# Summing the high and low parts of the PEER gates in PSUM: two 128-column products per token, one copy for four tokens

## The chip, the cores and the metric

One core of one Trainium2 chip runs the whole program. The metric is the device time of one execution in microseconds (us), the median of several runs. Engines are named as in the profile: PE is TensorE (its matrix products), PEld are PE's weight loads, DVE is VectorE, ACT is ScalarE, POOL is GpSimd, SP is SyncE, which issues most of the transfers.

## What is computed

The reference is two transformer blocks for 256 tokens of width 2048 in float32. The change touches the last layer, a PEER layer: every token picks 128 experts (8 heads of 16) out of 16384 = 128 x 128 by product keys, each with a gate, and sums their contributions.

```python
expert = jnp.take_along_axis(cand_idx, top_pos, axis=-1)
gate = jax.nn.softmax(top_s, axis=-1)
u = jnp.take(peer_u, expert, axis=0)
act = jax.nn.gelu(jnp.einsum('chkd,cd->chk', u, zc))
v = jnp.take(peer_v, expert, axis=0)
w = (gate * act.astype(jnp.float32)).astype(zc.dtype)
return jnp.einsum('chk,chkd->cd', w, v).astype(zc.dtype)
```

The kernel gathers nothing. It computes the gelu of **all** 16384 experts for all tokens (the stage that streams `peer_u`), builds a dense gate matrix with one 128 x 128 square of gates per token, multiplies the two, and forms the dense sum over all experts (the stage that streams `peer_v`).

## The kernel before

Every large weight matrix streams through the same loop (`Weights.take`, L125): SP loads 1 MB into one of 3 buffers `raw`; for each half of it, a chunk of 1024 columns, ACT writes the rounded high part `hi` (L140, format fp32r) and DVE the rest `lo` (L143), each into one of 4 buffers; then PE multiplies. A float32 product is made of three fp32r products: high by high, high by low, low by high (`unit_a`, L165 to L167). In the `peer_u` stage there are 32 units of 8 chunks. A chunk takes 24 products of 128 x 128 weights with 256 moving columns.

The gates are built beside this, as background work. `bg` is a list of (cost, function); after the split of each chunk, `take` calls `pump(1400)` (L144, L92), which takes entries from the front for as long as its budget is above 0 and subtracts each entry's cost:

```python
    def pump(budget):
        while bg and budget > 0:
            cost, fn = bg.popleft()
            fn()
            budget -= cost
```

So these costs decide how much gate work stands beside one chunk, and the scheduler then sets the order on each engine.

The gate work is done in 32 groups of 8 tokens. For a group, DVE makes four tiles of 1024 elements per partition, listed at a cost of 1250 each: `ha` (L1025, the one-hot rows of the first key), `he` (L1030, one-hot of the second key), and the two halves of `hb` (L1036, `he` times the high part and times the low part of the gates). In these tiles a partition is one of the token's 128 picked experts, so that the product of `ha` and `hb` over the partitions puts each gate at its place in the square. `meet` (L1038) makes that product on PE: one product per token, with `ha` of the token as weights and both parts of `hb` as 256 moving columns; a PSUM tile `gps` (one of 4 with the tag `tr`) takes two tokens. `store` (L1046) adds the two parts: ACT copies the high half to the tile `gst` (L1054) and DVE adds the low half to it (L1055), at a listed cost of 700. `gst` holds 32 tokens, in one of 2 buffers; after four groups a POOL-issued transfer writes it to memory (L1057). The entries are listed one group late: the products of group g stand between the one-hots of group g + 1 (L1059 to L1070). From the costs, a group before takes four calls of `pump`, so four chunks.

At the last unit (L1093) what is left of the list is emptied, and the `peer_v` stage reads the gates back.

Of the kernel before, what the change touches and what calls it, by code (L numbers as in the profile page):

```python
# [10 lines left out]
F32 = mybir.dt.float32  # L11
# [3 lines left out]
AF = mybir.ActivationFunctionType  # L15
ALU = mybir.AluOpType
# [29 lines left out]
def build(tc, t, out, dbg=None, stop=None):  # L46
# [4 lines left out]
    V, A, P, T = nc.vector, nc.scalar, nc.gpsimd, nc.tensor  # L51
# [36 lines left out]
    bg = deque()  # L88
# [199 lines left out]
    ps = tc.tile_pool(name="ps1", bufs=1, space=PSUM)  # L288
    psx = ExitStack()
    ps = psx.enter_context(ps)  # L290
# [51 lines left out]
    for g in range(4):  # L342
        z = xTs[g // 2][:, 4 * (g % 2):4 * (g % 2) + 4, :]
# [479 lines left out]
    for u in range(2):  # L823
# [3 lines left out]
        for g in (2 * u, 2 * u + 1):  # L827
# [7 lines left out]
            for jt in range(2):  # L835
                yp = ps.tile([128, 512], F32, tag="tr", name="yp", bufs=4)
                for i in range(2):
                    T.matmul(yp[:, :256], pw[:, g, i, 128 * jt:128 * jt + 128], dT[:, i, :],  # L838
                             start=(i == 0), stop=(i == 1))
                k = 2 * g + jt  # L840
# [14 lines left out]
    for n in range(4):  # L855
        acc = unit_b(ps, w, yh, yl, 16)
        for c in range(2):
            z = x2[:, c, 512 * n:512 * n + 512]
# [29 lines left out]
    st = [tk.tile([128, 16, 128], F32, name=f"st{c}") for c in range(2)]  # L888
# [113 lines left out]
    G = {}  # L1002
# [10 lines left out]
    NT = 8  # L1013
# [8 lines left out]
    def hot_a(g):  # L1022
        a = G["hot"].tile([128, 1152], F32R, tag="ha", name="ha")[:, 16:1040].rearrange("p (t k) -> p t k", t=NT)
        hot[g] = [a]
        V.tensor_tensor(a, iota8(), over(slotT[:, 0, :], g), op=ALU.is_equal)  # L1025

    def hot_e(g):
        e = G["hot"].tile([128, NT, 128], F32, tag="he", name="he", bufs=1)
        hot[g].append(e)
        V.tensor_tensor(e, iota8(), over(slotT[:, 1, :], g), op=ALU.is_equal)  # L1030

    def hot_b(g, i):
        if i == 0:
            hot[g].append(G["hot"].tile([128, NT, 2, 128], F32R, tag="hb", name="hb"))
        x = gateh.bitcast(F32) if i == 0 else gatel
        V.tensor_tensor(hot[g][2][:, :, i, :], hot[g][1], over(x, g), op=ALU.mult)  # L1036

    def meet(g, p):  # L1038

        a, _, b = hot[g]  # L1040
        o = ps.tile([128, 2, 2, 128], F32, tag="tr", name="gps", bufs=4)
        for j in range(2):
            T.matmul(o[:, j, :, :], a[:, 2 * p + j, :], b[:, 2 * p + j, :, :], start=True, stop=True)  # L1043
        hot[g, p] = o

    def store(g, p):  # L1046
        o = hot.pop((g, p))
        if g % 4 == 0 and p == 0:
            G["st"] = G["stage"].tile([128, NK, 32], F32, tag="gst", name="gst")
        k = NT * (g % 4) + 2 * p  # L1050
        z = G["st"][:, :, k:k + 2]
        h, l = o[:, :, 0, :], o[:, :, 1, :]
        h, l = h.rearrange("p t i -> p i t"), l.rearrange("p t i -> p i t")
        A.activation(z, h, AF.Copy)  # L1054
        V.tensor_tensor(z, l, z, op=ALU.add)  # L1055
        if g % 4 == 3 and p == NT // 2 - 1:
            nc.gpsimd.dma_start(gD[g // 4], G["st"].rearrange("p i t -> p (i t)"))  # L1057

    for g in range(S // NT + 1):  # L1059
        first, last = g == 0, g == S // NT  # L1060
        for i, fn in enumerate((lambda g=g: hot_a(g), lambda g=g: hot_e(g),
                                lambda g=g: hot_b(g, 0), lambda g=g: hot_b(g, 1))):
            if not last:
                bg.append((1250, fn))
            if not first:
                bg.append((0, lambda g=g, i=i: meet(g - 1, i)))
                if i:
                    bg.append((700, lambda g=g, i=i: store(g - 1, i - 1)))
        if not first:
            bg.append((700, lambda g=g: store(g - 1, 3)))  # L1070

    opt["budget"], opt["pool"] = 1400, 0
    wsp = lslot("lhi", "wsp", (4, 4, 256), off=16)
# [203 lines left out]
```

## Time and profile before

| | us |
|---|---|
| median of 3 runs | 2879.12 (2878.49 to 2879.72) |
| the profiled execution | 2881.8 |
| its span in the trace | 2880.0 |
| PE busy in the span | 2840.0 (99%) |
| DVE busy in the span | 1896.9 (66%) |
| ACT busy in the span | 1327.6 (46%) |

The profile shows one execution: each instruction with start, duration and what it waited for. A product's recorded duration covers its way through the array, and the next starts long before it ends; what PE spends on one is the distance between starts, called its step here. PE and PEld overlap in the same way.

### The profile page before, as it was taken

The numbers are of one execution on the slowest core, as the hardware profiler recorded it, in microseconds if no ns is written. First come the engines' busy times: TensorE is split into PE (matmuls) and PEld (weight loads), VectorE is DVE, ScalarE is ACT, GpSimd is POOL, SyncE is SP. The second block draws the span as 40 slices with busy tenths as digits, with TensorE's granted clock in tenths as the row PEclk, the third lists the DMA queues.
The fourth block names the chain that finished last, engine by engine and source line by source line (L and its number), as shares of the span: only waits on it lengthen the run. The fifth ranks groups of instructions, "written<-read, shape, count | busy, mean of one in ns | idle before, by whom it ended". The sixth has DMA issues, their size and how long they took to land.

```text
span 2880.0 us, 45191 instructions
## 1 busy us (share of the span) xinstructions
PE 2840.0 (99%) x18950; PEld 2596.6 (90%) x18950; DVE 1896.9 (66%) x2531; ACT 1327.6 (46%) x1638; POOL 33.0 (1%) x45
## 2 busy tenths in 40 slices
PE   8999999999999999999999999999999999999998
PEld 8887799999998888888999999999998888888886
DVE  7976665555554447856997988995445555555555
ACT  6226554444444445545444555544444444444443
POOL 0000000000000000000000000000000000000000
PEclk9999999999999999999999999999999999999999
DMA  6444555555565556465456667668667677767663
GB/s 239 165 148 145 205 199 197 191 193 195 198 220 190 194 197 219 147 219 212 173 214 221 227 231 263 231 256 300 219 219 277 236 241 244 241 239 247 236 223 141
DMA packets 120253, 615.72 MB, mean 214 GB/s; under 512 B 10320, under 2 KB 43216, under 8 KB 54768
## 3 DMA queue, kind: packets, MB, share of 16 engines
q1 hardware_dynamic: 116656, 574.16, 57.0%
q0 software_dynamic: 3392, 38.67, 3.4%
q8 instruction: 148, 2.42, 0.3%
q14 instruction: 57, 0.47, 0.0%
HBM read 570.85 MB, written 41.94 MB: 213 GB/s over the span
## 4 chain that ended last, share of the span: by engine, by line
PE 71%; issue 25%; DVE 3%; ACT 1%; DMA 0%; POOL 0%; SPq 0%; DVEq 0%; POOLq 0%
PE acc L167 16%; PE acc L166 16%; PE acc L165 16%; PE acc L180 6%; PE acc L179 6%; PE acc L181 6%; PE acc L189 3%; PE gps L1043 1%; DVE lo L143 1%; PE acc L198 0%; PE scp L922 0%; PE yp L838 0%; DMA raw<-w_in 0%; PE sp L515 0%; PE tsp L249 0%
## 5 line engine op out<-in xcount | busy, mean ns | idle before, releaser
L143 DVE TENSOR_TENSOR lo<-raw,hi 128x1024 fp32r<-128x1024 f32 (+1 forms) x968 | 1176.0, 1218 | 845.3 <-ACT hi L140 844.3
L140 ACT ACTIVATE hi<-raw 128x1024 fp32r<-128x1024 f32 (+1 forms) x968 | 1022.7, 1058 | 1345.6 <-PE acc L166 671.1
L167 PE MATMUL acc<-znh,lo 128*128 128x256 f32 x2048 | 564.7, 277 | 2.0 <-DVE lo L143 1.8
L165 PE MATMUL acc<-znh,hi 128*128 128x256 f32 x2048 | 565.5, 277 | 0.0
L166 PE MATMUL acc<-znl,hi 128*128 128x256 f32 x2048 | 565.5, 277 | 0.0
L1122 PE MATMUL o<-hi,wsp 128*128 128x512 f32 x2048 | 547.7, 389 | 0.0
L165 PE MATMUL acc<-lhi,hi 128*128 128x256 f32 x1856 | 514.6, 278 | 9.5 <-ACT hi L140 9.1
L166 PE MATMUL acc<-llo,hi 128*128 128x256 f32 x1856 | 514.6, 278 | 0.9 <-DVE llo L253 0.9
L167 PE MATMUL acc<-lhi,lo 128*128 128x256 f32 x1856 | 512.9, 277 | 1.3 <-DVE lo L143 1.2
L1122 PEld LDWEIGHTS o<-hi,wsp 128*128 128x128 f32 x2048 | 384.3, 188 | 79.8
L167 PEld LDWEIGHTS acc<-znh,lo 128*128 128x128 f32 x2048 | 383.3, 188 | 3.4 <-DVE lo L143 3.4
L165 PEld LDWEIGHTS acc<-znh,hi 128*128 128x128 f32 x2048 | 385.2, 188 | 0.0
L166 PEld LDWEIGHTS acc<-znl,hi 128*128 128x128 f32 x2048 | 384.5, 188 | 0.0
L165 PEld LDWEIGHTS acc<-lhi,hi 128*128 128x128 f32 x1856 | 350.4, 189 | 9.9 <-ACT hi L140 9.1
L166 PEld LDWEIGHTS acc<-llo,hi 128*128 128x128 f32 x1856 | 350.6, 189 | 1.4 <-DVE llo L253 1.4
L167 PEld LDWEIGHTS acc<-lhi,lo 128*128 128x128 f32 x1856 | 349.4, 189 | 2.2 <-DVE lo L143 2.2
L1122 PE MATMUL o<-lo,wsp 128*128 128x512 f32 x1024 | 315.4, 389 | 0.0
L1122 PEld LDWEIGHTS o<-lo,wsp 128*128 128x128 f32 x1024 | 192.2, 188 | 39.9
L180 PE MATMUL acc<-lo,acth 128*128 128x512 f32 x352 | 136.9, 389 | 0.0
L179 PE MATMUL acc<-hi,acth 128*128 128x512 f32 x352 | 136.9, 389 | 0.0
L181 PE MATMUL acc<-hi,actl 128*128 128x512 f32 x352 | 136.9, 389 | 0.0
L180 PE MATMUL acc<-lo,lhi 128*128 128x512 f32 (+1 forms) x352 | 136.7, 389 | 0.0
(338 smaller groups left out, 2728.0 us busy)
## 6 DMA issues: line engine op xcount, KB each, us to landing
raw<-peer_u SPq DMA_DIRECT2D x128, 1024.0 KB, 4.9
raw<-peer_v SPq DMA_DIRECT2D x128, 1024.0 KB, 5.9
raw<-w_gu SPq DMA_DIRECT2D x88, 1024.0 KB, 4.9
raw<-w_in SPq DMA_DIRECT2D x47, 1024.0 KB, 4.9
raw<-w_down SPq DMA_DIRECT2D x44, 1024.0 KB, 4.9
raw<-w_out SPq DMA_DIRECT2D x32, 1024.0 KB, 4.9
raw<-peer_wq SPq DMA_DIRECT2D x16, 1024.0 KB, 4.8
hD<-hg SPq DMA_DIRECT2D x32, 512.0 KB, 3.1
```

The lines of the kernel that those rows point to most:

```text
L140: A.activation(hi[:, :m], raw[:, o:o + m], AF.Copy)
L143: e.tensor_tensor(lo[:, :m], raw[:, o:o + m], hi[:, :m].bitcast(F32), op=ALU.subtract)
L165: T.matmul(o, hi[:, c], xh[:, kt, :], start=(kt == 0 and m % 2 == 0), stop=False)
L166: T.matmul(o, hi[:, c], xl[:, kt, :], start=False, stop=False)
L167: T.matmul(o, lo[:, c], xh[:, kt, :], start=False, stop=(kt == nkt - 1 and m % 2 == 1))
L179: T.matmul(o, xh[:, k, s], hi, start=(kt == 0), stop=False)
L180: T.matmul(o, xh[:, k, s], lo, start=False, stop=False)
L181: T.matmul(o, xl[:, k, s], hi, start=False, stop=(kt == nkt - 1))
L189: T.matmul(acc[m // 2][:, m % 2, :], v[:, m * 128:m * 128 + 128], x(kt), start=(kt == 0 and m % 2 == 0), stop=(kt == nkt - 1 and m % 2 == 1))
L1043: T.matmul(o[:, j, :, :], a[:, 2 * p + j, :], b[:, 2 * p + j, :, :], start=True, stop=True)
L1122: T.matmul(acc[c][o // 512 + q], x[:, s], v[:, 512 * q:512 * q + 512], start=st, stop=sp)
```

## The change

`meet` is called twice for a group instead of four times. It makes, for each of four tokens, two products of 128 moving columns, first with the high part and then with the low part of `hb`, which add up at the same place of a PSUM tile; the tile now holds four tokens. The weights of the two products are the same. `store` is one ACT copy of 512 elements per partition; DVE's addition is gone. The listed cost of `store` is 0 instead of 700.

```diff
@@ -1038,22 +1038,20 @@
     def meet(g, p):
 
         a, _, b = hot[g]
-        o = ps.tile([128, 2, 2, 128], F32, tag="tr", name="gps", bufs=4)
-        for j in range(2):
-            T.matmul(o[:, j, :, :], a[:, 2 * p + j, :], b[:, 2 * p + j, :, :], start=True, stop=True)
+        o = ps.tile([128, 4, 128], F32, tag="tr", name="gps", bufs=4)
+        for j in range(4):
+            for i in range(2):
+                T.matmul(o[:, j, :], a[:, 4 * p + j, :], b[:, 4 * p + j, i, :],
+                         start=(j == 0 and i == 0), stop=(j == 3 and i == 1))
         hot[g, p] = o
 
     def store(g, p):
         o = hot.pop((g, p))
         if g % 4 == 0 and p == 0:
             G["st"] = G["stage"].tile([128, NK, 32], F32, tag="gst", name="gst")
-        k = NT * (g % 4) + 2 * p
-        z = G["st"][:, :, k:k + 2]
-        h, l = o[:, :, 0, :], o[:, :, 1, :]
-        h, l = h.rearrange("p t i -> p i t"), l.rearrange("p t i -> p i t")
-        A.activation(z, h, AF.Copy)
-        V.tensor_tensor(z, l, z, op=ALU.add)
-        if g % 4 == 3 and p == NT // 2 - 1:
+        k = NT * (g % 4) + 4 * p
+        A.activation(G["st"][:, :, k:k + 4], o.rearrange("p t i -> p i t"), AF.Copy)
+        if g % 4 == 3 and p == 1:
             nc.gpsimd.dma_start(gD[g // 4], G["st"].rearrange("p i t -> p (i t)"))
 
     for g in range(S // NT + 1):
@@ -1062,12 +1060,12 @@
                                 lambda g=g: hot_b(g, 0), lambda g=g: hot_b(g, 1))):
             if not last:
                 bg.append((1250, fn))
-            if not first:
-                bg.append((0, lambda g=g, i=i: meet(g - 1, i)))
+            if not first and i % 2 == 0:
+                bg.append((0, lambda g=g, i=i: meet(g - 1, i // 2)))
                 if i:
-                    bg.append((700, lambda g=g, i=i: store(g - 1, i - 1)))
+                    bg.append((0, lambda g=g: store(g - 1, 0)))
         if not first:
-            bg.append((700, lambda g=g: store(g - 1, 3)))
+            bg.append((0, lambda g=g: store(g - 1, 1)))
 
     opt["budget"], opt["pool"] = 1400, 0
     wsp = lslot("lhi", "wsp", (4, 4, 256), off=16)
```

The scheduler places the rows of each engine. On DVE, in the middle of the gate stage, before; from one `he` (L1030) to the next is one group, with `lo` (L143) of the chunks of the weight stream between:

```order
L1030 TENSOR_TENSOR he<-cst,slotT 128x1024
L143 TENSOR_TENSOR lo<-raw,hi 128x1024 x2
L1055 TENSOR_TENSOR gst<-gps,gst 128x128x2 x2
L143 TENSOR_TENSOR lo<-raw,hi 128x1024
L1055 TENSOR_TENSOR gst<-gps,gst 128x128x2
L1025 TENSOR_TENSOR ha<-cst,slotT 128x1024
L1036 TENSOR_TENSOR hb<-he,gateh 128x8x128
L1036 TENSOR_TENSOR hb<-he,gatel 128x8x128
L143 TENSOR_TENSOR lo<-raw,hi 128x1024
L1055 TENSOR_TENSOR gst<-gps,gst 128x128x2
```

and now:

```order
L1025 TENSOR_TENSOR ha<-cst,slotT 128x1024
L143 TENSOR_TENSOR lo<-raw,hi 128x1024
L1030 TENSOR_TENSOR he<-cst,slotT 128x1024
L143 TENSOR_TENSOR lo<-raw,hi 128x1024
L1036 TENSOR_TENSOR hb<-he,gateh 128x8x128
L1036 TENSOR_TENSOR hb<-he,gatel 128x8x128
```

A group stood among four chunks of the stream and now stands among two; the four additions (L1055) are gone.

On PE, the products of the gates between two chunks, with buffer numbers, before (L1043):

```order
L167 MATMUL acc_15585<-znh_12208,lo_15623 128x256
L1043 MATMUL gps_15660<-hb_15549,ha_15479 128x256 x2
L1043 MATMUL gps_15665<-hb_15549,ha_15479 128x256 x2
L165 MATMUL acc_15584<-znh_12208,hi_15656 128x256
L166 MATMUL acc_15584<-znl_12209,hi_15656 128x256
```

and now (the same line is L1044 of the changed file):

```order
L165 MATMUL acc_15303<-znh_12208,hi_15476 128x256
L166 MATMUL acc_15303<-znl_12209,hi_15476 128x256
L167 MATMUL acc_15303<-znh_12208,lo_15477 128x256
L1044 MATMUL gps_15521<-hb_15406,ha_15363 128x128 x8
L165 MATMUL acc_15302<-znh_12208,hi_15517 128x256
```

The eight products of a group, of 256 columns, are now sixteen of 128 columns, in the same stream of products of 256 columns.

## Rows read from the trace of the kernel before

**Rows 1.** The page, parts 1 and 4: busy us of each engine, the chain's shares.
```profile
PE 2840.0 (99%) x18950; PEld 2596.6 (90%) x18950; DVE 1896.9 (66%) x2531; ACT 1327.6 (46%) x1638; POOL 33.0 (1%) x45
...
PE 71%; issue 25%; DVE 3%; ACT 1%; DMA 0%; POOL 0%; SPq 0%; DVEq 0%; POOLq 0%
```

**Rows 2.** Timeline of PE at the gate products: start us, us, and xcount merged.
```profile
1596.14 0.84 PE L1043 MATMUL gps<-hb,ha 128*128 128x256 f32 x6
1596.82 0.28 PE L167 MATMUL acc<-znh,lo 128*128 128x256 f32 x1
```

**Rows 3.** Stretches inside the peer_u stage: us, each engine's busy us (instructions), clock, DMA.
```profile
1700.00:1800.00 100.00, 100.00 (x885) 100.00 (x884) 89.34 (x103) 50.35 (x78) 1.06 (x2) 1.00 0.70 252
...
1965.00:2060.00 95.00, 95.00 (x840) 95.00 (x840) 49.23 (x41) 42.79 (x46) 0.00 (x0) 1.00 0.80 280
```

**Rows 4.** Timeline of POOL: two of the eight stores of gates.
```profile
1687.17 0.54 POOL L1057 DMA_DIRECT2D gD<-gst  x1 [46.36 <-DVE gst L1055]
1734.32 0.53 POOL L1057 DMA_DIRECT2D gD<-gst  x1 [46.60 <-DVE gst L1055]
```

**Rows 5.** Groups by line and shape, 1590 to 1965: busy us, mean ns, idle before.
```profile
L143 DVE TENSOR_TENSOR lo<-raw,hi 128x1024 fp32r<-128x1024 f32 x128 | 153.9, 1218 | 21.6 <-ACT hi L140 21.6
...
L1055 DVE TENSOR_TENSOR gst<-gps,gst 128x256 f32<-128x256 f32 x128 | 50.8, 420 | 0.0
L1054 ACT ACTIVATE gst<-gps 128x256 f32<-128x256 f32 x128 | 47.1, 400 | 0.0
...
L1036 DVE TENSOR_TENSOR hb<-he,gatel 128x1024 fp32r<-128x1024 f32 x32 | 39.0, 1218 | 0.0
L1036 DVE TENSOR_TENSOR hb<-he,gateh 128x1024 fp32r<-128x1024 f32 x32 | 39.0, 1217 | 0.0
L1030 DVE TENSOR_TENSOR he<-cst,slotT 128x1024 f32<-128x1024 f32 x31 | 37.6, 1214 | 0.0
L1025 DVE TENSOR_TENSOR ha<-cst,slotT 128x1024 fp32r<-128x1024 f32 x30 | 36.7, 1224 | 16.9 <-PE gps L1043 16.9
```

**Rows 6.** Waits, 1590 to 1965: us in total, times, longest us.
```profile
ACT hi L140 <- PE acc L166: 168.4, 111, 1.7
DVE lo L143 <- ACT hi L140: 21.6, 33, 1.4
```

**Rows 7.** Groups by line: ScalarE's copy of 512 elements out of PSUM, at the key scores.
```profile
L923 ACT ACTIVATE st<-scp 128x512 f32<-128x512 f32 x8 | 4.6, 598 | 4.7 <-PE scp L922 4.5
```

**Rows 8.** Timeline of PE in the last stage, 512 columns.
```profile
2300.07 1.07 PE L1122 MATMUL o<-hi,wsp 128*128 128x512 f32 x4
```

**Rows 9.** The page, part 5: the 512-column products and their weight loads.
```profile
L1122 PE MATMUL o<-hi,wsp 128*128 128x512 f32 x2048 | 547.7, 389 | 0.0
...
L1122 PEld LDWEIGHTS o<-hi,wsp 128*128 128x128 f32 x2048 | 384.3, 188 | 79.8
```

**Rows 10.** Timeline of PE at the key scores, plain f32 of 128 columns.
```profile
1370.51 1.95 PE L922 MATMUL scp<-kk,qTu 128*128 128x128 f32 x16
```

**Rows 11.** Timeline of PE around four one-column records of plain f32.
```profile
36.85 0.39 PE L167 MATMUL acc<-lhi,lo 128*128 128x256 f32 x2
37.08 0.50 PE L336 MATMUL rtk<-ones,xsq 128*128 128x1 f32 x4
37.44 0.36 PE L165 MATMUL acc<-lhi,hi 128*128 128x256 f32 x1
37.65 0.28 PE L166 MATMUL acc<-llo,hi 128*128 128x256 f32 x1
```

**Rows 12.** Timeline of PE's weight loads in the same stretch.
```profile
36.97 0.53 PEld L336 LDWEIGHTS rtk<-ones,xsq 128*128 128x128 f32 x4
```

**Rows 13.** DMA issues of the whole run: xcount, KB each, median us to landing.
```profile
raw<-peer_u SPq DMA_DIRECT2D x128, 1024.0 KB, 4.9
...
gD<-gst POOLq DMA_DIRECT2D x8, 2048.0 KB, 12.3
```

## The prediction

> **What bounds the kernel now.** I read the page first, then stretches of the stage in which the change lies, then the groups, waits and timelines of that stage. PE is busy for 99% of the span and the chain of waits runs through PE, with DVE at 3% and ACT at 1% of it [rows 1]. Busy time of PE alone proves little, since its records overlap, so the step matters, the distance between two starts. In the gate stage six gate products start between 1596.14 and 1596.82 [rows 2]: 0.68 / 6 = 0.1133 us for a product of 256 columns. After the stage 840 products lie in 95 us [rows 3], 0.1131 us each. So with the gate work beside it PE ran as densely as without it; no stall of PE is left there for the change to win back.
>
> A group of gates before takes four chunks: 4 x 24 x 0.1133 + 8 x 0.1133 = 10.88 + 0.91 = 11.79 us of PE. Two stores of gates, four groups apart, are 1734.32 - 1687.17 = 47.15 us apart [rows 4], which is 4 x 11.79: PE sets the pace exactly. DVE is close behind it. Per group it has four `lo` (1.218 us), one each of `ha`, `he` and the two `hb` (1.224 + 1.214 + 1.217 + 1.218 = 4.87 us) and four additions of 0.420 us [rows 5]: 4.87 + 4.87 + 1.68 = 11.43 us, and 89.34 of 100 us busy in mid-stage [rows 3]. What DVE idles there, it waits for others: 16.9 us before `ha` for PE [rows 5], 21.6 us before `lo` for ACT, which waits for PE to free `hi` [rows 6]. It is slack, though little.
>
> **What goes: DVE and ACT work.** 128 additions of 0.420 us leave DVE, 53.8 us. 128 copies of 0.400 us leave ACT [rows 5] and 64 of 512 elements come; the nearest row, a copy of the same size out of PSUM, took 0.598 us [rows 7]: 51.2 us becomes 38.3 us. Neither was on the path, so I price both gains at nothing. ACT is half idle in the stage [rows 3]; per group it will have two `hi` and two copies, about 3.3 us of 7.3 us.
>
> **What comes: the products on PE.** 256 products of 256 columns become 512 of 128. The old ones took 256 x 0.1133 = 29.0 us. The trace has no fp32r product under 256 columns, so the step has to be bounded.
> - From below: half of 0.1133 us, if columns alone counted. Then 512 x 0.0567 = 29.0 us, a difference of 0. Columns do set the step of long products: four of 512 columns take 1.07 us [rows 8] with a record of 0.389 us [rows 9], so (1.07 - 0.389) / 3 = 0.227 us, twice that of 256.
> - From above: a plain f32 product of 128 columns, which leaves two records. Sixteen records take 1.95 us [rows 10]; less a last record of some 0.28 us, 1.67 / 15 = 0.111 us each, 0.223 us a product. Then 114.2 us, a difference of +85.
> - Between them: every product loads its own weights. The page counts 2048 loads for 2048 products, though in that line two neighbours share their weights [rows 9]; so the second product of a token will load again. How fast loads follow one another is seen where columns cost nothing: two products of a single column, four records, stand among the stream. From 36.85 to 37.65 there are two stream records, the four, and one more [rows 11]: 0.80 / 7 = 0.114 us each, no faster than 256 columns. The four loads take 0.53 us [rows 12], with 0.188 us for one [rows 9]: (0.53 - 0.188) / 3 = 0.114 us apart. I take 0.112 us, between this and the 0.111 us of the 128-column records: the weight load sets the floor, and halving the columns buys nothing.
>
> So PE gets 512 x 0.112 = 57.3 us for 29.0 us: **+28.3 us**, on the bounding engine, with nothing to hide it.
>
> The Trainium skill (TensorE: Matmul & The Clock Gate, section Back-to-back issue gap) gives about 81 ns per product at 128 columns and about 131 ns at 512 for a sustained stream of load and product pairs. As an estimate by its 81 ns, PE's term would be 512 x 0.081 - 29.0 = +12.5 us, and the time 2892 us if PE alone set it. The trace differs from that section where both can be compared: 512 columns take 227 ns here [rows 8], so the row decides.
>
> **What moves: the pace of the gate work.** With `store` listed at 0, a group takes two calls of the pump instead of four, and the order on DVE shows it: two `lo` beside the four gate tiles. DVE then needs 2 x 1.218 + 4.87 = 7.31 us per group, and PE 2 x 24 x 0.1133 + 16 x 0.112 = 5.44 + 1.79 = 7.23 us. DVE, ahead before, becomes the slower by a hair. Paced by DVE the 32 groups take 233.9 us. The same 64 chunks with the old products were 64 x 2.72 + 29.0 = 203.1 us of PE. That is **+30.8 us**: PE's +28.3 us and 2.5 us of waiting for `lo` or `hb`. It also means that a quicker product helps little: anything under 0.117 us (7.31 - 5.44 = 1.87 us over 16) is paced by DVE. The other 64 chunks of the old stage run afterwards at PE's bare 2.72 us, so nothing is lost or won there.
>
> On the queues the work comes closer together. The store of gates on POOL lands in 12.3 us [rows 13] and comes every 4 x 7.31 = 29.2 us, with two `gst` buffers. SP's 1 MB loads land in 4.9 us [rows 13] and are wanted once per 7.31 us. The copies queue in front of `hi` on ACT and wait for the products, but four `hi` buffers lie between. I price these at nothing; without that cover, they would add to rival one.
>
> The sum against the profiled execution: 2881.8 + 30.8 = 2912.6 us. It stands 2.7 us above the median of the runs, so 2879.1 + 30.8, about **2910 us**, 1.1% slower. A measurement of this kernel can tell about 0.2% (5.8 us) from no change. The forecast's own range is 2905 (PE alone, a step of 0.109 us) to 2916 (0.114 us, and a few us of waits).
>
> **Rivals.**
> 1. DVE's waits stay. It waited 16.9 us in total for PE before `ha` [rows 5]; before, that was slack. If it waits as long with DVE setting the pace, the group takes 7.31 + 0.53 = 7.84 us, and 32 x 7.84 - 203.1 = +47.8 us: 2927. For it: the two engines are nearly level, and each waits for the other in turn. Against: there are two `ha` buffers, so a `ha` needs only the products of the group before last to be done. Chance 0.10.
> 2. fp32r under 256 columns runs as plain f32, in two passes: 0.223 us [rows 10], +85 us, 2964. Against: the fp32r rows cost what their columns cost, and nothing in the trace shows a second kind. Chance 0.06.
> 3. The products go at the columns' rate, 0.0567 us, and DVE's lead covers part of its pace. The lead is at most four `lo` tiles, 4 x 2.72 = 10.9 us, of 30.8 us: at least +20 us, 2899. The weight loads [rows 11, 12] speak against it. Chance 0.04.
> 4. Not slower. The same quick products, and DVE no longer binding: PE needs 5.44 + 0.91 = 6.35 us per group, so this decides from 6.35 / 6 = 1.06 us per DVE operation downwards, now that the additions have gone. Time 2879. DVE's tiles of this size took 1.214 to 1.224 us, all of them [rows 5]. Chance 0.02.
>
> **How the numbers follow.** Forecast 0.78, rivals 0.10, 0.06, 0.04 and 0.02. The range, 2902 to 2928, holds the forecast with its bounds and reaches up to rival 1; it leaves out rivals 2 to 4, 0.12, and some tail. All cases but rival 4 are slower by more than 0.2%: slower 0.98, same 0.01, faster 0.01.
>
> **What would show it.** Gate products of 128 columns with steps near 0.112 us, PEld as dense as PE, and 512 of each. Stores of gates some 29 us apart: 29.0 means PE's pace (7.23 x 4 = 28.9), 29.2 DVE's, 31.4 rival 1, 36 rival 2 (4 x 9.0), 25.4 rival 4. DVE near 100% busy for some 234 us from 1596, and the stage then running bare to its end. The prediction is wrong if the step lies far from 0.112 us while the time is as forecast (then DVE was the bound), or if the stage shows PE waiting much longer than 5 us in all.

## The result and the profile after

The changed kernel took 2909.26 us (2908.40 to 2909.83, 4 runs) against 2879.42 us of the kernel before (4 runs beside it): a ratio of 1.0103, 95% interval 1.0091 to 1.0115. That is 29.8 us more, in the range of the prediction and 0.7 us under its figure. The profiled executions differ less, 2908.4 against 2881.8 us, because that of before lies 2.7 us above its median and that of after 0.9 us under its own. Most of that lies ahead of the first gate product (see the last section).

The page of the changed kernel, parts 1 and 4:

```profile
PE 2866.7 (99%) x19206; PEld 2623.8 (90%) x19206; DVE 1860.3 (64%) x2403; ACT 1322.7 (46%) x1574; POOL 33.0 (1%) x45
...
PE 71%; issue 24%; DVE 2%; ACT 1%; DMA 1%; POOL 0%; SPq 0%; DVEq 0%; POOLq 0%
```

Against [rows 1], PE has 19206 - 18950 = 256 more products and as many more weight loads, and 26.7 us more busy time; DVE has 36.6 us less, ACT 4.9 us less. The chain still runs through PE at 71%, and DVE's share of it went from 3% to 2%: what DVE and ACT were relieved of shows in their busy time and hardly on the path.

The timeline of PE at the gate products (start us, us, records merged):

```profile
1649.44 0.90 PE L1044 MATMUL gps<-hb,ha 128*128 128x128 f32 x7
1650.18 0.33 PE L167 MATMUL acc<-znh,lo 128*128 128x256 f32 x1
1650.35 0.28 PE L165 MATMUL acc<-znh,hi 128*128 128x256 f32 x1
```

This answers to [rows 2]. Seven products of 128 columns start at 1649.44; the next product of the stream starts at 1650.18 and the one after it at 1650.35. Those eight, seven short ones and one of 256 columns, take 0.91 us, 0.114 us each. In [rows 2] the same engine spent 0.1133 us on twice the columns.

Stretches of the stage (us, then busy us of PE, PEld, DVE, ACT and POOL with instructions, clock, DMA):

```profile
1620.00:1800.00 180.00, 180.00 (x1588) 180.00 (x1587) 173.28 (x150) 84.22 (x112) 3.20 (x6) 1.00 0.65 240
1840.00:1960.00 120.00, 120.00 (x1061) 120.00 (x1061) 57.51 (x48) 52.96 (x57) 0.00 (x0) 1.00 0.69 243
```

PE is full in the gate stage and behind it, as in [rows 3], at 180 / 1588 = 0.1134 and 120 / 1061 = 0.1131 us per product. But of every 64 products 16 now belong to the gates, where it was 8 of 104.

The stores of gates on POOL:

```profile
1646.70 0.54 POOL L1055 DMA_DIRECT2D gD<-gst  x1 [28.66 <-ACT gst L1053]
...
1762.88 0.53 POOL L1055 DMA_DIRECT2D gD<-gst  x1 [28.48 <-ACT gst L1053]
```

Four stores, sixteen groups, lie in 1762.88 - 1646.70 = 116.18 us: 29.05 us per store and 7.26 us per group, where [rows 4] gave 47.15 us and 11.79 us. Two chunks of the stream are 5.44 us of it, so 16 products took 1.82 us, **0.114 us each**.

Groups of the gate stage by line and shape, 1590 to 1820 (xcount, busy us, mean ns of one, idle before):

```profile
L143 DVE TENSOR_TENSOR lo<-raw,hi 128x1024 fp32r<-128x1024 f32 x64 | 78.3, 1223 | 11.4 <-ACT hi L140 11.2
...
L1044 PE MATMUL gps<-hb,ha 128*128 128x128 f32 x512 | 65.8, 267 | 0.0
L1044 PEld LDWEIGHTS gps<-hb,ha 128*128 128x128 f32 x512 | 63.3, 191 | 0.0
L1036 DVE TENSOR_TENSOR hb<-he,gatel 128x1024 fp32r<-128x1024 f32 x32 | 39.0, 1220 | 0.0
L1053 ACT ACTIVATE gst<-gps 128x512 f32<-128x512 f32 x64 | 37.9, 593 | 14.1 <-PE gps L1044 14.1
...
L1025 DVE TENSOR_TENSOR ha<-cst,slotT 128x1024 fp32r<-128x1024 f32 x30 | 36.8, 1226 | 0.3
```

Against [rows 5], the additions are gone and the copies of 512 elements took 593 ns, as [rows 7] had it. DVE's 16.9 us of waiting for PE before `ha` has become 0.3 us. Its wait for `hi` before `lo`, 21.6 us for 128 `lo` in [rows 6], is 11.2 us for 64: DVE still idles. The timeline of DVE shows how long one of its tiles holds it:

```profile
1645.81 1.22 DVE L1025 TENSOR_TENSOR ha<-cst,slotT 128x1024 fp32r<-128x1024 f32 x1
1646.95 1.22 DVE L143 TENSOR_TENSOR lo<-raw,hi 128x1024 fp32r<-128x1024 f32 x1
1648.09 1.22 DVE L1030 TENSOR_TENSOR he<-cst,slotT 128x1024 f32<-128x1024 f32 x1
1649.57 1.23 DVE L143 TENSOR_TENSOR lo<-raw,hi 128x1024 fp32r<-128x1024 f32 x1 [0.27 <-ACT hi L140]
1650.71 1.22 DVE L1036 TENSOR_TENSOR hb<-he,gateh 128x1024 fp32r<-128x1024 f32 x1
1651.85 1.22 DVE L1036 TENSOR_TENSOR hb<-he,gatel 128x1024 fp32r<-128x1024 f32 x1
```

The records last 1.22 us, but two that follow without a wait start 1.14 us apart (1646.95 to 1648.09, 1650.71 to 1651.85). So DVE's records overlap, as those of PE do, and the step of such a tile is 1.14 us.

### The profile page after: what moved, and what is told of

The parts are those of the page before. It is cut to its first block, busy times and chain, and to the rows that moved or that the text cites. A ratio compares the mean times of both kernels' runs of the same rounds, so it can differ in the third digit from the quotient of the medians.

```text
span 2906.6 us, 45562 instructions
## 1 busy us (share of the span) xinstructions
PE 2866.7 (99%) x19206; PEld 2623.8 (90%) x19206; DVE 1860.3 (64%) x2403; ACT 1322.7 (46%) x1574; POOL 33.0 (1%) x45
## 4 chain that ended last, share of the span: by engine, by line
PE 71%; issue 24%; DVE 2%; ACT 1%; DMA 1%; POOL 0%; SPq 0%; DVEq 0%; POOLq 0%
PE acc L165 16%; PE acc L167 16%; PE acc L166 16%; PE acc L181 6%; PE acc L180 6%; PE acc L179 6%; PE acc L189 2%; PE gps L1044 2%; DVE lo L143 1%; DMA raw<-w_out 0%; ACT hi L140 0%; PE scp L922 0%; PE yp L838 0%; PE acc L198 0%; DMA raw<-w_in 0%
## 5 line engine op out<-in xcount | busy, mean ns | idle before, releaser
L143 DVE TENSOR_TENSOR lo<-raw,hi 128x1024 fp32r<-128x1024 f32 (+1 forms) x968 | 1180.0, 1220 | 937.0 <-ACT hi L140 935.5
```

The costliest lines, as they stand in the source:

```text
L143: e.tensor_tensor(lo[:, :m], raw[:, o:o + m], hi[:, :m].bitcast(F32), op=ALU.subtract)
```

## The experiments

Three readings were set against each other. **W**: a product's step at 128 columns is set by the load of its weights, so the added products cost all of the loss. **D**: the gate work was squeezed between two chunks and DVE sets the pace there. **C**: columns alone count, and the loss has another cause. The diff of the first run is against the kernel before, those of the others against the changed kernel.

### The split alone

```diff
         for j in range(2):
-            T.matmul(o[:, j, :, :], a[:, 2 * p + j, :], b[:, 2 * p + j, :, :], start=True, stop=True)
+            for i in range(2):
+                T.matmul(o[:, j, i, :], a[:, 2 * p + j, :], b[:, 2 * p + j, i, :],
+                         start=(j == 0 and i == 0), stop=(j == 1 and i == 1))
```

> The kernel before, with only the products split: each product of 256 columns is two of 128 columns with the same weights, into the two halves of the same tile; copy, addition, listed costs and the pace of four chunks per group stay. Theory W (the weight load sets a product's step, about 0.112 us at 128 columns): 512 x 0.112 - 29.0 = +28 us, ratio 1.010, about 2908 us; stores of gates 4 x (10.88 + 1.79) = 50.7 us apart. Theory D (the change is slower because the gate work was squeezed among two chunks and DVE sets the pace there): nothing is squeezed here, ratio 1.000 to 1.002. Theory C (columns alone count, step 0.057 us): ratio 1.000.

Measured: ratio 1.0104 (1.0087 to 1.0121), 2910.56 us, the whole of the loss with nothing of the rest of the change. Its stores of gates:

```profile
1693.52 0.54 POOL L1059 DMA_DIRECT2D gD<-gst  x1 [50.04 <-DVE gst L1057]
1744.34 0.53 POOL L1059 DMA_DIRECT2D gD<-gst  x1 [50.28 <-DVE gst L1057]
```

50.82 us apart, against 47.15 us in [rows 4]: 3.67 us for 32 products more, 0.115 us for each added one. C falls on this run, and so does D as the cause of the loss, since nothing was squeezed here. Whether DVE costs the changed kernel 2 or 3 us on top is left to the runs below.

### The pace alone

```diff
-        o = ps.tile([128, 4, 128], F32, tag="tr", name="gps", bufs=4)
-        for j in range(4):
-            for i in range(2):
-                T.matmul(o[:, j, :], a[:, 4 * p + j, :], b[:, 4 * p + j, i, :],
-                         start=(j == 0 and i == 0), stop=(j == 3 and i == 1))
-        hot[g, p] = o
+        hot[g, p] = []
+        for q in range(2):
+            o = ps.tile([128, 2, 2, 128], F32, tag="tr", name="gps", bufs=4)
+            for j in range(2):
+                n = 4 * p + 2 * q + j
+                T.matmul(o[:, j, :, :], a[:, n, :], b[:, n, :, :], start=True, stop=True)
+            hot[g, p].append(o)
...
-        A.activation(G["st"][:, :, k:k + 4], o.rearrange("p t i -> p i t"), AF.Copy)
+        for q in range(2):
+            A.activation(G["st"][:, :, k + 2 * q:k + 2 * q + 2],
+                         o[q][:, :, 0, :].rearrange("p t i -> p i t"), AF.Copy)
```

> The changed kernel's listing with the old products: 256 columns per token, two tokens per tile, two copies per store and no addition; the low part is left out of the sum (it is computed on PE, not copied). The order on DVE gives 2.5 chunks per group on average. Theory W: PE does what it did before, 2.5 x 2.72 + 0.91 = 7.71 us per group, and nothing else counts: ratio 1.000, 2879 to 2881 us. Theory D: DVE at 1.22 us for each of 6.5 tiles needs 7.93 us per group, so 32 x 0.22 = +7 us, ratio 1.0025 or more. Theory C says as W.

Measured: 0.9996 (0.9987 to 1.0006), 2880.19 us. Taking the additions away and drawing the gate work together, here among 2.5 chunks a group and not 2, neither gains nor costs anything that the interval shows, and D's 1.0025 lies outside it.

### Twice as many products again

```diff
             for i in range(2):
-                T.matmul(o[:, j, :], a[:, 4 * p + j, :], b[:, 4 * p + j, i, :],
-                         start=(j == 0 and i == 0), stop=(j == 3 and i == 1))
+                for s in (slice(0, 64), slice(64, 128)):
+                    T.matmul(o[:, j, s], a[:, 4 * p + j, :], b[:, 4 * p + j, i, s],
+                             start=(j == 0 and i == 0 and s.start == 0),
+                             stop=(j == 3 and i == 1 and s.start == 64))
```

> The changed kernel with each product of 128 columns made as two of 64 columns, 1024 in all, same weights. Theory W: 1024 x 0.112 - 29.0 = +86 us over before, ratio 1.030, about 2965 us. If a product costs columns plus a fixed part (0.112 = 0.053 + 0.059), 64 columns cost 0.086 us: 88 - 29 = +59 us, ratio 1.020. Theory C: as the changed kernel, 1.010. Theory D: the pace of DVE hides it only up to 0.117 us per two products, so it says nothing of its own here.

Measured: 1.0314 (1.0297 to 1.0332), 2972.23 us, so +90.4 us. A fixed part plus columns (1.020) is excluded; the 1024 products cost as much each as the 512. The 4 to 5 us over W's 86 us can be found in the trace:

```profile
1600.00:1604.00 4.00, 4.00 (x23) 4.00 (x23) 3.44 (x4) 0.94 (x2) 0.00 (x0) 0.57 0.46 195
1604.00:1608.00 4.00, 4.00 (x38) 4.00 (x37) 2.60 (x3) 2.39 (x4) 0.00 (x0) 1.00 0.36 128
1872.00:1876.00 4.00, 4.00 (x38) 4.00 (x37) 1.23 (x1) 2.02 (x3) 0.00 (x0) 1.00 0.48 199
1876.00:1880.00 4.00, 4.00 (x24) 4.00 (x24) 0.00 (x0) 0.60 (x1) 0.53 (x1) 0.59 0.15 66
```

In the profiled execution the granted clock fell twice to its lower level (1.2 GHz) for some 3 us, with 0.57 and 0.59 on average in these stretches and 1.00 beside them. Each time PE had just made a long row of gate products of 64 columns, 28 and 48 of them one behind the other, where a row has 16 in most groups. That cost 15 and 14 products of the stream, 3.3 us. The rest is the step, which is 0.1133 us and not W's 0.112: 1024 x 0.1133 - 29.0 = +87.0 us, with 3.3 us +90.3 us.

### One DVE tile more per group

```diff
-        V.tensor_tensor(e, iota8(), over(slotT[:, 1, :], g), op=ALU.is_equal)
+        for _ in range(2):
+            V.tensor_tensor(e, iota8(), over(slotT[:, 1, :], g), op=ALU.is_equal)
```

> The changed kernel with one more DVE tile per group (the one-hot of the second key is made twice). The order on DVE gives 8/3 chunks per group. PE needs 2.67 x 2.72 + 16 x 0.1133 = 9.07 us per group. Theory W (PE alone; DVE's step from start to start is 1.135 us in the trace, so 7.67 x 1.135 = 8.70 us): as the changed kernel, ratio 1.010, within 2 us of it. Theory D (1.22 us a tile, 7.67 x 1.22 = 9.35 us, 0.28 us per group over PE): +9 us on the changed kernel, ratio 1.0135.

Measured: 1.0107 (1.0090 to 1.0124), 2911.83 us, as the changed kernel. The stores tell more sharply than the time:

```profile
1666.47 0.54 POOL L1056 DMA_DIRECT2D gD<-gst  x1 [35.90 <-ACT gst L1054]
...
1775.57 0.53 POOL L1056 DMA_DIRECT2D gD<-gst  x1 [36.14 <-ACT gst L1054]
```

Three intervals between stores, twelve groups, take 109.10 us, 9.09 us per group: PE's 9.07 us, not D's 9.35 us. With 32 more DVE tiles the stage still ran at PE's pace.

### A slower pace for the same work

```diff
-                    bg.append((0, lambda g=g: store(g - 1, 0)))
+                    bg.append((1400, lambda g=g: store(g - 1, 0)))
...
-            bg.append((0, lambda g=g: store(g - 1, 1)))
+            bg.append((1400, lambda g=g: store(g - 1, 1)))
```

> The changed kernel with the listed cost of a store at 1400 instead of 0, so that a group stands among three chunks instead of two; the work is the same. Theory W (PE alone, 0.113 us for each of 512 loads): as the changed kernel, ratio 1.010. Theory D (DVE set the changed kernel's pace): with 7 tiles per group for three chunks DVE has slack even at 1.22 us (8.54 against 9.97 us of PE), so 2 to 3 us less than the changed kernel, ratio 1.0095 or less.

Measured: 1.0101 (1.0086 to 1.0117), 2910.10 us. It agrees with W; the interval is too wide to exclude D's 1.0095 by itself.

### Half the columns, the same number of products

```diff
-            for i in range(2):
-                T.matmul(o[:, j, :], a[:, 4 * p + j, :], b[:, 4 * p + j, i, :],
-                         start=(j == 0 and i == 0), stop=(j == 3 and i == 1))
+            T.matmul(o[:, j, :], a[:, 4 * p + j, :], b[:, 4 * p + j, 0, :], start=(j == 0), stop=(j == 3))
```

> The changed kernel with the product of the high part alone: 256 products of 128 columns, half the columns of the kernel before; the low part of the gates is left out of the sum. Theory W: 256 loads as before, 256 x 0.112 = 28.7 us for 29.0 us, ratio 1.000, 2879 to 2882 us. Theory C (columns count): 256 x 0.057 = 14.5 us, ratio 0.995, about 2866 us. 2.5 chunks per group keep DVE out of it: 6.5 x 1.135 = 7.38 us against 7.7 us of PE under theory W.

Measured: 1.0002 (0.9993 to 1.0011), 2882.21 us. Half of the gate columns of the kernel before are gone and nothing is gained; C's 0.995 lies far outside. In fp32r the number of products, each with its load, sets the time, here 256 as before.

Loads and products are equal in number in all these runs, so the counts alone can't tell the load from another fixed cost of an fp32r product. The timeline of the changed kernel speaks for the load. Here one gate product stands alone in the stream (PE first, then the loads):

```profile
1648.39 0.22 PE L1044 MATMUL gps<-hb,ha 128*128 128x128 f32 x1
1648.45 0.33 PE L165 MATMUL acc<-znh,hi 128*128 128x256 f32 x1
1648.62 0.28 PE L166 MATMUL acc<-znl,hi 128*128 128x256 f32 x1
```

```profile
1648.28 0.19 PEld L1044 LDWEIGHTS gps<-hb,ha 128*128 128x128 f32 x1
1648.39 0.19 PEld L165 LDWEIGHTS acc<-znh,hi 128*128 128x128 f32 x1
1648.50 0.19 PEld L166 LDWEIGHTS acc<-znl,hi 128*128 128x128 f32 x1
1648.62 0.19 PEld L167 LDWEIGHTS acc<-znh,lo 128*128 128x128 f32 x1
```

The product behind it starts after 0.06 us, about what 128 columns cost at the rate of the 512-column products (0.227 / 4 = 0.057 us). But its record is 0.05 us longer than its neighbours', and the one behind it starts only after 0.17 us, while the loads keep steps of 0.11 to 0.12 us. So the short product gave PE free early, and what it saved was lost again to the pace of the loads. The ends of PE's records are modelled, and no run made several products from one load: this is an argument, not a proof.

### The same products in bf16

```diff
-        a = G["hot"].tile([128, 1152], F32R, tag="ha", name="ha")[:, 16:1040].rearrange("p (t k) -> p t k", t=NT)
+        a = G["hot"].tile([128, 1152], BF16, tag="ha", name="ha")[:, 16:1040].rearrange("p (t k) -> p t k", t=NT)
...
-            hot[g].append(G["hot"].tile([128, NT, 2, 128], F32R, tag="hb", name="hb"))
-        x = gateh.bitcast(F32) if i == 0 else gatel
+            hot[g].append(G["hot"].tile([128, NT, 2, 128], BF16, tag="hb", name="hb"))
+        x = gateh if i == 0 else gatel
```

The high part `gateh` is in bf16 as well (one ScalarE copy writes it), and `gatel` is the rest.

> The changed kernel with the operands of the gate products in bf16 instead of fp32r: the one-hots exactly, the gates as a bf16 high part and the rest rounded to bf16. Same 512 products of 128 columns. If the load's time hangs on the operand's width (theory W with a load of about half, step 0.057 to 0.060 us): 512 x 0.058 = 29.7 us, ratio 1.000, about 2881 us; DVE at 1.135 us stays under PE on average (6.4 x 1.135 = 7.26 us against 7.45 us), with up to 5 us of waiting where only two chunks stand beside a group. If a load costs 0.11 us whatever the type: 1.010.

Measured: 1.0082 (1.0068 to 1.0095), 2904.90 us. Neither number: by the time alone the load seems to cost the same in bf16. The timeline says otherwise:

```profile
1656.50 0.96 PE L1046 MATMUL gps<-hb,ha 128*128 128x128 bf16 x14
1657.27 0.37 PE L167 MATMUL acc<-znl,hi 128*128 128x256 f32 x1
1657.47 0.28 PE L168 MATMUL acc<-znh,lo 128*128 128x256 f32 x1
```

Fourteen products and one of the stream take 1657.47 - 1656.50 = 0.97 us. With 0.118 us for the last, 0.85 / 14 = 0.061 us each: the bf16 product costs half of the fp32r one. (The 14 start 0.77 / 14 = 0.055 us apart; the rest is the way back to fp32r.) Its weight load, in the groups by line (xcount, busy us, mean ns):

```profile
L1046 PE MATMUL gps<-hb,ha 128*128 128x128 bf16 x512 | 40.1, 220 | 0.0
...
L1046 PEld LDWEIGHTS <-ha 128*128 128x128 bf16 x512 | 28.9, 98 | 2.6
```

is 98 ns long, where the fp32r one was 191 ns. Whether the load or the columns, at 0.057 us for 128, set the step in bf16 can't be told from this: the two are equal. What took the gain away lies in the products that were not changed. Stretches behind the gate stage, of this run and then of the kernel before:

```profile
1840.00:2160.00 320.00, 320.00 (x2719) 320.00 (x2718) 145.25 (x119) 137.31 (x144) 0.00 (x0) 1.00 0.64 227
```

```profile
1965.00:2160.00 195.00, 195.00 (x1723) 195.00 (x1723) 94.44 (x78) 87.25 (x92) 0.00 (x0) 1.00 0.71 249
```

PE is full in both, with the clock at 1.00 and no gate product in sight, but a product of the stream takes 320 / 2719 = 0.1177 us in one and 195 / 1723 = 0.1132 us in the other. Behind its last gate product, at 1833, this run has 3054 products of the stream; at 4.5 ns more each, that is 13.7 us. The gate stage, 240.5 us from its first gate product to its last, holds 1786 products of the stream. With the 256 gate products of the kernel before these would take (1786 + 256) x 0.1133 = 231.4 us, so the stage lost 9.1 us: 512 x 0.061 - 29.0 = +2 us for the gates and 7 us for the stream, which took the slower step in 18 of its 33 longer stretches (ten products or more) between gate products. Together that is 22.8 us, and 23.3 us were measured.

### bf16, the high part alone

The kernel of the run above, with its gate products cut as in the run on half the columns:

```diff
-            for i in range(2):
-                T.matmul(o[:, j, :], a[:, 4 * p + j, :], b[:, 4 * p + j, i, :],
-                         start=(j == 0 and i == 0), stop=(j == 3 and i == 1))
+            T.matmul(o[:, j, :], a[:, 4 * p + j, :], b[:, 4 * p + j, 0, :], start=(j == 0), stop=(j == 3))
```

> As the run in bf16, with the product of the high part alone: 256 products of 128 columns in bf16; the low part of the gates is left out, so the gates have bf16's precision. If the width sets the load: 256 x 0.058 = 14.8 us, 14 us less than before, ratio 0.995, about 2866 us. If a load costs 0.11 us whatever the type: 1.000.

Measured: 1.0026 (1.0015 to 1.0036), 2889.64 us, +8.1 us. Again the stream is slower behind the gate stage:

```profile
1860.00:2160.00 300.00, 300.00 (x2549) 300.00 (x2548) 136.66 (x112) 129.63 (x137) 0.00 (x0) 1.00 0.64 224
```

300 / 2549 = 0.1177 us. The same account: 2816 products behind the last gate product cost 12.7 us more. The gate stage takes 253.3 us for 2024 products of the stream, against (2024 + 256) x 0.1133 = 258.3 us, so 5.0 us less: the gates save 14 us (256 x 0.057 us, the distance of their starts in this trace, instead of 29.0 us) and the stream, slower in 26 of its 32 longer stretches, gives 9 us of that back. Together +7.7 us. No version that was run beats the kernel before.

## Why the prediction was right, and where it was not

- **What bounds the kernel, and what goes.** PE before and after; 53.8 us of DVE's work and the copies of ACT brought nothing. The run with the pace alone shows it for the additions, 0.9996; that the split alone, with the old copies and additions, costs as much as the whole change, 1.0104 and 1.0103, shows it for both.
- **The products on PE.** The term was +28.3 us at 0.112 us a product. The stores of gates give 0.114 us, so 512 x 0.114 - 29.0 = +29.4 us. The split alone gave +28.7 us against the runs beside it, all of the loss within the error. So the term was 1.1 us too small. The argument from the single-column products was the right one; the two bounds, 0 and +85 us, were both far off, and rival 2 (two passes) and rivals 3 and 4 (quick products) with them. Of the two readings of the sum, the row was nearer than the 81 ns of the Trainium skill (TensorE: Matmul & The Clock Gate, section Back-to-back issue gap): no fp32r product here, at 64, 128 or 256 columns, had a mean step under 0.11 us.
- **The pace of DVE: this step failed.** I wrote that DVE "becomes the slower by a hair", at 7.31 us per group, and added 2.5 us of waiting. The 7.31 us summed record durations of 1.22 us. The start-to-start step is 1.14 us, so six tiles are 6.8 us, below PE's 7.26 us, and DVE kept its slack: 11.2 us of waiting for `hi` in the stage. The trace of before showed it already, had I taken DVE's timeline and not the mean durations; I had done just that for PE:

```profile
1705.48 1.23 DVE L1025 TENSOR_TENSOR ha<-cst,slotT 128x1024 fp32r<-128x1024 f32 x1 [0.62 <-PE gps L1043]
1706.63 1.22 DVE L1036 TENSOR_TENSOR hb<-he,gateh 128x1024 fp32r<-128x1024 f32 x1
1707.76 1.22 DVE L1036 TENSOR_TENSOR hb<-he,gatel 128x1024 fp32r<-128x1024 f32 x1
1708.90 1.22 DVE L143 TENSOR_TENSOR lo<-raw,hi 128x1024 fp32r<-128x1024 f32 x1
1710.03 0.43 DVE L1055 TENSOR_TENSOR gst<-gps,gst 128x256 f32<-128x256 f32 x1
1710.37 1.22 DVE L1030 TENSOR_TENSOR he<-cst,slotT 128x1024 f32<-128x1024 f32 x1
```

A tile takes 1.14 us from start to start and an addition 0.34 us, so DVE needed 8 x 1.14 + 4 x 0.34 = 10.5 us of the 11.79 us per group, and not the 11.43 us of the prediction. The sign that I had named (29.0 us between stores for PE's pace, 29.2 us for DVE's) pointed to PE with the measured 29.05 us, but is too fine to decide. The DVE tile more per group decides: it would have cost 9 us by my sum, and it cost nothing that the interval shows. The other sign, DVE near 100% busy, was no sign at all: its records fill 173.28 of 180 us although it waits in most groups, because they overlap.
- **"A quicker product helps little"** rested on the same sum. With 6.84 us on DVE's side its limit is (6.84 - 5.44) / 16 = 0.088 us a product instead of 0.117 us. So more could have been won than I wrote, down to that; a product at the columns' rate of 0.057 us would still have been paced by DVE in two chunks a group. What did stand in the way of quicker products in bf16 was another thing, which I had no row for.
- **Rival 1**, DVE's waits staying: the wait before `ha` went to 0.3 us.
- That the total came out within a microsecond is partly luck: PE's term was a microsecond too small and DVE's term 2.5 us too large, so the figure is nearer than its parts.

## What to carry to other kernels

Price a product by the distance between starts, and ask whether columns or the weight load sets it: here fp32r products of 256, 128 and 64 columns all cost 0.113 us, most likely the pace of their loads, so splitting one product into two doubles it, and dropping half of its columns gains nothing. Sums in PSUM are paid for in products; they can be worth it only where the engine that is relieved sets the pace, which DVE did not here; such a case was not run. The same caution holds for DVE: the records of its tiles of 1024 elements overlap by some 0.08 us, and a bound summed from durations is that much too high per instruction.

## What the runs showed of the hardware that was not expected

The stream of fp32r products of 256 columns has two steps at the same granted clock of 1.00: 0.1132 us and 0.1177 us, and it holds either for hundreds of microseconds (320 us in the bf16 run above). In the kernel before, the slower one holds for a stretch ahead of the gate stage:

```profile
1540.08 0.28 PE L166 MATMUL acc<-znl,hi 128*128 128x256 f32 x1
...
1541.14 0.28 PE L166 MATMUL acc<-znl,hi 128*128 128x256 f32 x1
```

There nine products take 1.06 us, 0.118 us each, and at 1596 in [rows 2] the step is 0.1133 us again. The two levels also come without a difference in the gate work, which begins behind this stretch (the kernel before, then the changed one):

```profile
1500.00:1590.00 90.00, 89.12 (x758) 88.50 (x757) 71.31 (x91) 40.37 (x44) 0.00 (x0) 1.00 0.62 221
1500.00:1590.00 90.00, 89.12 (x779) 88.43 (x779) 73.64 (x94) 41.41 (x45) 0.00 (x0) 1.00 0.62 220
```

The 21 products more are 2.4 us, and that is about what the profiled execution of before lost against its median. The traces of five other runs show 757 or 758 products there, those of three others 779. With one trace of each kernel it can't be told whether the program or the single execution decides; the times of the kernel before beside the experiments, 2878.3 to 2883.4 us, leave room for the second.

Which of the two follows a short product, a wait or a change of type was not settled. After the gate products in bf16 the slower one came in 18 of 33 and 26 of 32 stretches and stayed to the end of the stage in both runs. After those in fp32r it came for a few products at most in nearly all stretches, and behind the gate stage the faster one held. Nothing was run to force one or the other, so what sets it stays open.
